# A mixture-of-experts stage in whole weight units: the down product moves behind the next slot's gate and up

## The chip, the cores and the metric

The kernel runs on one core of a Trainium2 chip. The metric is the device time of one execution in microseconds (us), the median of three runs. The weights lie in HBM in float32, and the result has to be of nearly float32 quality, which sets how the matrix products are made (below).

## The reference, cut to what matters

Two layers act on 512 latent tokens; the first also carries 256 context tokens, so its expert stage has 768 tokens and that of layer two 512. Each layer is a mixer (layer one: a gated linear recurrence beside differential attention; layer two: windowed attention) and then a routed mixture of 16 experts, of which every token takes two. The change is in this stage alone:

```python
D_MODEL = 1024; N_EXPERTS = 16; TOP_K = 2; D_EXPERT = 1024

def routed_moe(h2d, router_w, router_b, w_gate, w_up, w_down):
    aff = jax.nn.sigmoid(jnp.dot(h2d, router_w).astype(F32))
    ...                                  # two experts of the best group of four, normed weights wts
    def expert_block(args):              # a block: up to 128 rows of one expert e
        xblk, e = args
        hid = jax.nn.silu(xblk @ w_gate[e]) * (xblk @ w_up[e])
        return hid @ w_down[e]
    yb = lax.map(expert_block, (xb, block_e)).reshape(n_rows, d_)
    out = jnp.zeros((n_tok + 1, d_), F32).at[row_tok].add(yb * row_w[:, None])
```

Every expert's three matrices (1024x1024 float32, 4 MB each) are used in both layers: 192 MB a layer, read once.

## The kernel before, in words

**Slots.** The stage of a layer runs over 16 slots, one expert each. Slot 0 is an expert that is known before the routing; the others are ranked by load. A slot's number of rows is fixed when the kernel is built (`PLANS`): 128, 64, or 128 and a further block of 32. Rows that find no place go to a loop, `tc.For_i(0, n_ov)`, whose count `n_ov` is read at run time (`values_load(nov)`). With these inputs it runs zero times, but every engine loads the count and branches, and before that each waits until the other engines and all transfers that were issued so far are done.

**Weights.** A slot has 12 units of 1 MB, of 128 partitions x 2048: 4 of gate, 4 of up, 4 of down. SyncE (SP) issues their loads (`load_raw`) into raw buffers of several pools (`ROOM` gives the pools' sizes, the strings `FIRST` and `ROUND` name the pool for each unit in turn). A load waits until its buffer is free.

**Products.** For a block of 128 rows a unit is split into two float32r parts: ScalarE (ACT) writes `wh` (a copy, L193), VectorE (DVE) writes `wl` = raw - wh (L195), two such pairs of 1024 columns to a unit. TensorE (PE) then makes three products for each 128x512 piece, `mm3` (L208, L209, L210). So a 128-row slot has 96 of them for gate and up (on `xh`, `xl`) and 48 for down (on `hh`, `hl`), beside 16 transposes. A block of 64 or 32 rows takes the raw weights as they are (`thin`, L1219, on `xn`, then `hn`).

**Order in a slot.** Gate and up are made in two halves of 512 columns: steps 0 to 3 read all 8 units, two a step, for columns 0 to 511, and steps 4 to 7 read the same 8 units for columns 512 to 1023. A unit's raw buffer is free after the second. After each half `hidden` makes silu(gate) * up (L1336, L1337), transposes it on PE (L1201) and splits it into `hh` and `hl` (L1205, L1206). Steps 8 to 11 are the down product of the same slot, then `result` weights the rows and POOL stores them to `YD` (L1431). The rows of the next slot are gathered by POOL (`fetch`, L1184), transposed on PE and split in the slot before.

**Start and end.** 12 units are loaded ahead of the routing's result (`AHEAD`). After that step 15 (slot 0 and three steps of slot 1) the loop stands. Behind slot 14 the rows in YD are gathered for the output (`fetch_y`, L1131), slot 15 goes to the output by a product with a selection matrix (L1447).

Of the kernel before, what the change touches and what calls it, by code (L numbers as in the profile page):

```python
# [9 lines left out]
FT = mybir.dt.float32  # L10
FR = mybir.dt.float32r
# [20 lines left out]
ROOM = [(5, 1, 3), (2, 4, 1, 3)]  # L32
BRIEF = [True, False]
# [5 lines left out]
LOOP_POOL = [2, 3]  # L39


class Plan:
# [21 lines left out]
    Plan([(128,)] * 3 + [(64,), (128,)] * 6 + [(64,)]),  # L64
# [48 lines left out]
def body(tc, a):  # L113
# [8 lines left out]
    with ExitStack() as top:  # L122
# [996 lines left out]
        def ffn(li, nt, xs, keep, project, after_project, at_end):  # L1119
# [39 lines left out]
            with ExitStack() as es:  # L1159
# [31 lines left out]
                def loop_pool():  # L1191
                    return room[LOOP_POOL[li]]


# [28 lines left out]
                def run(experts, blocks, sizes):  # L1223
# [12 lines left out]

                    def gather(p, first, step):
# [3 lines left out]
                        def get():  # L1241
                            if in_loop:
                                p["ix"] = wk.tile([128, 1], I32, name="ix")
                                p["sw"] = wk.tile([128, 1], FT, name="sw")
                                V.tensor_copy(p["ix"], rowi[:, ds(b + NB - 1, 1)])
                                V.tensor_copy(p["sw"], roww[:, ds(b + NB - 1, 1)])
                                p["xg"] = fetch(p["ix"][:, 0:1])
                                return
                            p["sw"] = (roww if m == 128 else again[m][:, 1])[:, b:b + 1]
                            p["ix"] = (rowi if m == 128 else again[m][:, 0])[:, b:b + 1]  # L1250
                            p["xg"] = fetch(rowi[:m, b:b + 1], p["n"] % 2 == 0, m)

                        def turn(q):
# [3 lines left out]
                            if q == 0 and in_loop:  # L1257
                                p["xh"] = (keep if one else wk2).tile([128, 8, 128], FR, name=f"xhl{li}", tag="xl0" if one else "y", bufs=1 if one else 2)
                                p["xl"] = wk2.tile([128, 8, 128], FR, name="xll", tag="y", bufs=1 if one else 2)
                            elif q == 0:  # L1260
                                for x in ("xh", "xl"):
                                    p[x] = wk2.tile([128, 8, 128], FR, name=x, bufs=1 if one else 2)
# [14 lines left out]
                    slots, n = [], 0  # L1277
                    for s in range(len(experts)):
                        slots.append([])
                        for b, m in zip(blocks[s], sizes[s]):  # L1280
                            r0 = (b + NB - 1) * 128 if in_loop else b * 128
                            row = (lambda i, k, r0=r0: ds(r0, 128)) if in_loop else (lambda i, k, r0=r0: slice(r0 + i, r0 + i + k))
                            slots[-1].append(dict(b=b, m=m, n=n, row=row))
                            n += 1
                    total = 12 * len(slots)
                    ahead, raws, regs = {}, {}, {}

                    def expert(s):
                        e = experts[s]
                        if callable(e):  # L1290
                            e = regs[s] = regs[s] if s in regs else e()
                        return e

                    def load(u, eng=nc.sync, order=False):
                        s, q = divmod(u, 12)
                        w = (wg, wu, wd)[q // 4][ds(expert(s), 1)].rearrange("o (u p j) n -> p (o u) (j n)", p=128, j=2)
                        k = len(FIRST[li])
                        pool = 0 if in_loop else int(FIRST[li][u] if u < k else ROUND[li][(u - k) % len(ROUND[li])])
                        raw = load_raw(w[:, q % 4], loop_pool() if in_loop else wx if pool == 9 else room[pool], eng, order)
                        return raw.rearrange("p (j n) -> p j n", j=2)  # L1300

                    def part(m, kh, c):

                        w = (wg, wu)[m][ds(expert(0), 1)].rearrange("o (u p j) n -> p (o u) j n", p=128, j=2)
                        raw = loop_pool().tile([128, 2048], FT, name="raw", tag="raw").rearrange("p (k n) -> p k n", k=4)
                        for x in range(2):
                            nc.sync.dma_start(raw[:, 2 * x:2 * x + 2], w[:, 2 * kh + x, :, 512 * c:512 * c + 512])
                        return raw

                    def unit(u):  # L1310
                        if u not in raws:
                            raws[u] = ahead.pop(u) if u in ahead else load(u)
                        return raws[u]

                    def weights(i):
# [7 lines left out]
                        if in_loop:  # L1323
                            return split(part(m, kh, c)), []
                        rs = [unit(12 * s + 4 * m + 2 * kh + x) for x in range(2)]
                        return [w for r in rs for w in split(r[:, :, 512 * c:512 * c + 512])], rs

                    def hidden(p, c, step):

                        pg, pu = p["ps"]  # L1330

                        def vec():
                            if c == 0:
                                p["h"] = [wk.tile([128, 8, 128], FR, name=x, bufs=1) for x in ("hh", "hl")]
                            sg = wk.tile([128, 512], FT, name="sg", bufs=1 if one else 2)
                            S.activation(sg, pg, AF.Silu)  # L1336
                            V.tensor_mul(sg, sg, pu)  # L1337
                            p["sg"] = sg
# [4 lines left out]
                        def store():  # L1343
                            parts(p["pt"], *(x[:, 4 * c:4 * c + 4] for x in p["h"]))

                        if step is None:
                            vec()
                            turn()
                            store()
                        else:  # L1350
                            at(step, False, vec)
                            at(step, True, turn)
                            at(step + 1, False, store)

                    def hidden_thin(p, step):

# [595 lines left out]
```

## Time and profile before

| | |
|---|---|
| median of three runs | 2195.73 us (2192.98 to 2196.71) |
| the profiled execution | 2198.97 us, span 2197.3 us |
| granted TensorE clock, mean | 0.961 |
| PE, DVE, ACT busy | 91%, 65%, 52% of the span |
| DMA | 569.22 MB, 259 GB/s over the span |
| expert stage of layer one | about 581 us (first unit load) to 1261 us |
| expert stage of layer two | about 1609 us (first unit load) to 2197 us |

The profile is of one execution. It has rows of 40 equal slices of the span (each 54.9 us) with the busy share of each engine in tenths, the clock that PE was granted (1.00 is 2.4 GHz, half of it 1.2 GHz), and what the 16 DMA engines moved. The other views are a table of stretches of time, the waits of one engine by what ended them, and lists of instructions in order of time.

### The profile page before, as it was taken

How to read it: one execution, taken by the hardware profiler on the slowest of the kernel's cores; microseconds unless marked ns; L12 is line 12 of the kernel's file. 1: busy time of each engine (PE TensorE's matmuls, PEld its weight loads, DVE VectorE, ACT ScalarE, POOL GpSimd, SP SyncE). 2: the span in 40 equal slices, each digit the busy share in tenths (PEclk: the TensorE clock that was granted, in tenths of full speed). 3: DMA queues.
4: the chain of work that ended last, by engine and by line, in shares of the span. 5: the costliest groups of instructions: out<-in, count | busy, mean ns of one | idle time of the engine just before them, and what ended most of it. 6: DMA issues, size and time to landing. Idle time of an engine off the chain costs nothing. (4 is left out here: it accounts for less than half of the span.)

```text
span 2197.3 us, 31173 instructions
## 1 busy us (share of the span) xinstructions
PE 1997.5 (91%) x11439; PEld 1505.1 (68%) x11439; DVE 1429.6 (65%) x2283; ACT 1144.3 (52%) x1816; POOL 207.1 (9%) x269
## 2 busy tenths in 40 slices
PE   4899999998968999999999889999967999999996
PEld 2777898997746887767778467566745865556653
DVE  3656746667677987857789465565576954556653
ACT  5444474443235886757678262565335743354541
POOL 1211110000110000000000330000010000000002
PEclk8899999999978999999999989999988999999998
DMA  8865333213456899899989842440428999999996
GB/s 306 284 208 197 90 96 100 75 47 104 176 212 236 362 401 355 335 402 396 356 330 383 306 133 102 172 162 1 146 110 317 377 414 412 413 412 413 412 417 191
DMA packets 128230, 569.22 MB, mean 259 GB/s; under 512 B 12790, under 2 KB 48640, under 8 KB 72440
## 3 DMA queue, kind: packets, MB, share of 16 engines
q1 hardware_dynamic: 103104, 485.36, 56.7%
q0 software_dynamic: 17856, 66.71, 9.2%
q10 hardware_dynamic: 7112, 15.10, 2.1%
q8 instruction: 93, 1.52, 0.3%
q14 instruction: 65, 0.53, 0.1%
HBM read 540.01 MB, written 38.12 MB: 263 GB/s over the span
## 5 line engine op out<-in xcount | busy, mean ns | idle before, releaser
L195 DVE TENSOR_TENSOR wl<-raw,wh 128x1024 fp32r<-128x1024 f32 (+1 forms) x606 | 722.8, 1219 | 160.0 <-ACT wh L193 149.5
L193 ACT ACTIVATE wh<-raw 128x1024 fp32r<-128x1024 f32 (+1 forms) x606 | 629.6, 1054 | 269.8 <-PE acc L210 206.0
L209 PE MATMUL acc<-wl,xh 128*128 128x512 f32 x736 | 300.5, 408 | 35.5 <-DVE wl L195 32.5
L208 PE MATMUL acc<-wh,xh 128*128 128x512 f32 x736 | 296.8, 406 | 13.1 <-ACT wh L193 13.1
L210 PE MATMUL acc<-wh,xl 128*128 128x512 f32 x736 | 295.1, 401 | 0.0
L208 PE MATMUL acc<-wh,hh 128*128 128x512 f32 (+2 forms) x716 | 271.7, 379 | 4.3 <-ACT hh L476 3.9
L210 PE MATMUL acc<-wh,hl 128*128 128x512 f32 (+2 forms) x716 | 265.1, 371 | 0.3 <-DVE hl L477 0.3
L209 PE MATMUL acc<-wl,hh 128*128 128x512 f32 (+2 forms) x716 | 264.8, 370 | 0.0
L209 PEld LDWEIGHTS acc<-wl,xh 128*128 128x128 f32 x736 | 143.2, 195 | 76.1 <-DVE wl L195 37.1
L208 PEld LDWEIGHTS acc<-wh,xh 128*128 128x128 f32 x736 | 143.2, 195 | 57.3 <-ACT wh L193 22.5
L210 PEld LDWEIGHTS acc<-wh,xl 128*128 128x128 f32 x736 | 143.2, 195 | 29.4 <-DVE xl L1206 0.5
L208 PEld LDWEIGHTS acc<-wh,hh 128*128 128x128 f32 x716 | 137.1, 191 | 25.4 <-ACT hh L476 4.3
L210 PEld LDWEIGHTS acc<-wh,hl 128*128 128x128 f32 x716 | 136.1, 190 | 21.7 <-DVE hl L477 0.8
L209 PEld LDWEIGHTS acc<-wl,hh 128*128 128x128 f32 x716 | 136.7, 191 | 18.3
L1219 PE MATMUL acc<-raw,xn 128*64 128x512 f32 (+1 forms) x832 | 141.3, 529 | 0.0
L1219 PEld LDWEIGHTS acc<-raw,xn 128*64 128x64 f32 (+1 forms) x832 | 48.0, 128 | 86.8 <-issue 77.5
L1184 POOL DMA_INDIRECT xg<-H,rowi x32 | 42.0, 1314 | 637.0 <-PE tp L1201 570.4
L1219 PE MATMUL acc<-raw,hn 128*64 128x512 f32 (+1 forms) x416 | 75.4, 540 | 10.6 <-DMA raw<-in_moe_w_down_dram 6.8
L1363 DVE TENSOR_TENSOR sg<-sg,acc 128x512 f32<-128x512 f32 (+1 forms) x11 | 7.0, 638 | 119.5 <-PE acc L1219 119.5
L152 POOL TENSOR_TENSOR rr<-rv,mhalf 128x1 f32<-128x1 f32 (+1 forms) x54 | 37.1, 687 | 481.4 <-DVE rv L150 463.7
L1205 ACT ACTIVATE xh<-tp 128x512 fp32r<-128x512 f32 x46 | 27.0, 588 | 99.2 <-PE tp L1201 99.2
L1047 DVE TENSOR_REDUCE mx<-big 128x1 f32<-128x512 f32 (+1 forms) x64 | 48.1, 756 | 37.1 <-PE big L1045 36.4
(416 smaller groups left out, 3296.4 us busy)
## 6 DMA issues: line engine op xcount, KB each, us to landing
raw<-in_moe_w_gate_dram SPq DMA_DIRECT2D x128, 1024.0 KB, 10.7
raw<-in_moe_w_up_dram SPq DMA_DIRECT2D x128, 1024.0 KB, 13.0
raw<-in_moe_w_down_dram SPq DMA_DIRECT2D x127, 1024.0 KB, 14.5
raw<-in_ada_w_dram SPq DMA_DIRECT2D x48, 1024.0 KB, 6.2
YD<-y POOLq DMA_DIRECT2D x23, 512.0 KB, 8.1
YD<-YD POOLq DMA_DIRECT2D x21, 512.0 KB, 11.9
raw<-in_even_w_in_dram SPq DMA_DIRECT2D x40, 256.0 KB, 4.5
raw<-in_even_w_in_dram SPq DMA_DIRECT2D x12, 512.0 KB, 4.6
```

The lines of the kernel that those rows point to most:

```text
L152: G.tensor_tensor(r, v, mhalf[:, :n], OP.pow)
L193: S.activation(v[0], src, AF.Copy)
L195: newest[0] = V.tensor_sub(v[1], src, v[0].bitcast(FT))
L208: T.matmul(o, xh, wh, start=start, stop=False)
L209: T.matmul(o, xh, wl, start=False, stop=False)
L210: T.matmul(o, xl, wh, start=False, stop=stop)
L1047: V.tensor_reduce(mx[:, i:i + 1], ps[:, :n], AX.X, OP.max, negate=True)
L1184: i = G.indirect_dma_start(out=xg[:rows], out_offset=None, in_=H[:, :], in_offset=bass.IndirectOffsetOnAxis(ap=ix, axis=0))
L1205: S.activation(oh, pt, AF.Copy)
L1219: T.matmul(ps[m * r:m * r + m, :n], x, w[:, n * r:n * r + n], start=start, stop=stop, tile_position=(0, m * r))
L1363: V.tensor_mul(sg, sg, pu[:, :8 * m])
```

## The change

A step is one whole unit: each of its two 128x1024 parts goes into two PSUM banks, one for each half of the columns (`thick`). The steps stand in the list `seq`: gate and up of slot s (8 steps), then down of slot s-1 (4 steps); at the end down of slot 14, gate and up of slot 15, down of slot 15. `hh`, `hl` and `hn` get two buffers; `xh` and `xl`, of which layer one had two, get one. SP loads 11 units ahead in layer one (8 of gate and up, 3 of down) and 12 in layer two; before, POOL issued the twelfth of layer one. The loop stands after step 4 of slot 0, and its body is written out on its own (`overflow`). Layer two's slots were 128 rows x 3, (64, 128) x 6, 64; they are 128, (64, 128) x 6, 128 x 2, 64: as many of each size.

```diff
-ROOM = [(5, 1, 3), (2, 4, 1, 3)]
-FIRST = ["000091113331100001111291", "0093110022224440011002222"]
-ROUND = ["00009111112", "934440011002222"]
-AHEAD = [(range(11), range(11, 12)), (range(12), range(0))]
-LOOP_AFTER = [range(15, 21), range(15, 25)]
+ROOM = [(5, 1), (2, 1, 4, 2)]
+FIRST = ["9200001192000011111", "920000114492000033331144920000"]
+ROUND = ["92000011111", "33331144920000"]
+AHEAD = [[*range(8), *range(16, 19)], [*range(8), *range(16, 20)]]
+LOOP_STEP = 4
...
-    Plan([(128,)] * 3 + [(64,), (128,)] * 6 + [(64,)]),
+    Plan([(128,)] + [(64,), (128,)] * 6 + [(128,)] * 2 + [(64,)]),
...
+                def thick(ps, kk, hi, lo, ws, w=512):
+                    wh, wl = ws
+                    for x in range(2):
+                        cs = slice(w * x, w * x + w)
+                        mm3(ps[x], hi[:, kk], lo[:, kk], wh[:, cs], wl[:, cs], kk == 0, kk == 7)
...
+                        if s == 15:
+                            seq += [(14, q) for q in range(8, 12)]
+                        seq += [(s, q) for q in range(8)]
+                        if 0 < s < 15:
+                            seq += [(s - 1, q) for q in range(8, 12)]
+                    seq += [(15, q) for q in range(8, 12)]
...
                     def weights(i):
-                        s, q = divmod(i, 12)
-                        m, kh, c = q // 2 % 2, q % 2, q // 4
-                        if slots[s][0]["m"] < 128:
-                            return [], [unit(i)]
-                        if q >= 8:
-                            return split(unit(i)), [unit(i)]
-                        rs = [unit(12 * s + 4 * m + 2 * kh + x) for x in range(2)]
-                        return [w for r in rs for w in split(r[:, :, 512 * c:512 * c + 512])], rs
+                        raw = ahead.pop(i) if i in ahead else load(i)
+                        return split(raw) if slots[seq[i][0]][0]["m"] == 128 else [], raw
...
-                                p["h"] = [wk.tile([128, 8, 128], FR, name=x, bufs=1) for x in ("hh", "hl")]
+                                p["h"] = [wk.tile([128, 8, 128], FR, name=x) for x in ("hh", "hl")]
...
-                            turns.append(12 * s - 5 + 2 * x if one else max(12 * s - 5 + 2 * x, 10))
-                            gather(p, max(turns[-3] + 2, 16) if p["n"] > 1 else 4, turns[-1])
+                            turns.append(6 if s == 1 else g - 3 + 2 * x)
+                            gather(p, LOOP_STEP if p["n"] == 1 else max(turns[-3] + 2, 9), turns[-1])
...
+                            for x, p in enumerate(slots[s]):
+                                if q == 7 and p["m"] == 128:
+                                    hidden(p, 0, i + 1)
+                                    hidden(p, 1, i + 2)
...
-                steps(11)
-                early_units[0](LOOP_AFTER[li])
-                steps(15)
+                steps(LOOP_STEP)
                 n_ov = nc.values_load(nov[0:1, 0:1], min_val=0, max_val=OVMAX)
                 in_loop = all_in_wx[0] = True
                 with tc.For_i(0, n_ov, 1) as j:
-                    finish(run([lambda: nc.sync.value_load(eoi[0:1, ds(j, 1)], min_val=0, max_val=15)], [[j]], [(128,)]))
+                    overflow(j)
                 in_loop = all_in_wx[0] = False
+                if one:
+                    steps(10)
+                    gates()
```

In `weights`, before, `m`, `kh` and `c` are gate or up, the half of the rows, and the half of the columns.

A scheduler sets the final order on each engine. The first place is SP at the loop in layer two. Before, these rows stand there: the 12 units ahead, the expert number of slot 1 (`esi`), 9 loads of slot 1 and 4 of slot 2 (left out), and then the count.

```order
L164 DMA raw<-in_moe_w_gate_dram 128x2048 x4
L164 DMA raw<-in_moe_w_up_dram 128x2048 x4
L164 DMA raw<-in_moe_w_down_dram 128x2048 x4
L1757 TENSOR_LOAD esi
...
L164 DMA raw<-in_moe_w_gate_dram 128x2048
L1812 TENSOR_LOAD nov
L1814 COMPARE_AND_BRANCH
```

Now the count stands right behind the 12 units, and the expert number of slot 1 with its 8 loads of gate and up comes behind the loop:

```order
L162 DMA raw<-in_moe_w_gate_dram 128x2048 x4
L162 DMA raw<-in_moe_w_up_dram 128x2048 x4
L162 DMA raw<-in_moe_w_down_dram 128x2048 x4
L1781 TENSOR_LOAD nov
L1783 COMPARE_AND_BRANCH
...
L1781 ISA x2
L1736 TENSOR_LOAD esi
L1736 ISA x2
L162 ISA
L162 DMA raw<-in_moe_w_gate_dram 128x2048
```

In layer one the count moved in the same way on SP. On PE it moved up by nine steps: 72 products of slot 0 stand ahead of it in layer one (gate, and half of up) and 96 in layer two (all of gate and up of slot 0), where before the count stood in slot 1.

The second place is DVE in a 128-row slot of layer one, early in the stage. Before, the four products for `sg` and `hl` of a slot lie in two places, 14 and 6 splits apart:

```order
L195 TENSOR_TENSOR wl<-raw,wh 128x1024 x14
L1337 TENSOR_TENSOR sg<-sg,acc 128x512
L195 TENSOR_TENSOR wl<-raw,wh 128x1024 x2
L1206 TENSOR_TENSOR hl<-tp,hh 128x512
L195 TENSOR_TENSOR wl<-raw,wh 128x1024 x6
L1206 TENSOR_TENSOR xl<-tp,xh 128x512
L1337 TENSOR_TENSOR sg<-sg,acc 128x512
L195 TENSOR_TENSOR wl<-raw,wh 128x1024 x2
L1206 TENSOR_TENSOR xl<-tp,xh 128x512
L1206 TENSOR_TENSOR hl<-tp,hh 128x512
```

Now 16 splits stand in a row, and the six others all lie among the next eight, those of the four down units:

```order
L193 TENSOR_TENSOR wl<-raw,wh 128x1024 x16
L1380 TENSOR_TENSOR sg<-sg,acc 128x512
L193 TENSOR_TENSOR wl<-raw,wh 128x1024 x2
L1380 TENSOR_TENSOR sg<-sg,acc 128x512
L193 TENSOR_TENSOR wl<-raw,wh 128x1024 x2
L1200 TENSOR_TENSOR hl<-tp,hh 128x512
L193 TENSOR_TENSOR wl<-raw,wh 128x1024 x2
L1200 TENSOR_TENSOR xl<-tp,xh 128x512
L1200 TENSOR_TENSOR hl<-tp,hh 128x512
L193 TENSOR_TENSOR wl<-raw,wh 128x1024 x2
L1200 TENSOR_TENSOR xl<-tp,xh 128x512
```

## Rows read from the trace of the kernel before

**Rows 1.** The page: what the DMA moved in 40 slices of the span.

```profile
GB/s 306 284 208 197 90 96 100 75 47 104 176 212 236 362 401 355 335 402 396 356 330 383 306 133 102 172 162 1 146 110 317 377 414 412 413 412 413 412 417 191
```

**Rows 2.** Windows of stages: length, busy us of each engine, clock, DMA share, GB/s.

```profile
708.00:1223.00 515.00, 510.65 (x2587) 396.98 (x2588) 418.51 (x400) 377.74 (x424) 33.19 (x38) 0.99 0.93 370
...
1752.00:2109.00 357.00, 338.69 (x1507) 208.35 (x1506) 194.60 (x201) 157.16 (x180) 24.16 (x27) 0.98 1.01 413
```

**Rows 3.** Windows: one 128-row slot of layer one.

```profile
778.20:813.30 35.10, 35.10 (x162) 28.84 (x161) 31.80 (x30) 28.77 (x33) 2.02 (x2) 1.00 1.00 403
```

**Rows 4.** Windows: one of four like pairs, a 128-row and a 64-row slot, layer two.

```profile
1848.00:1913.20 65.20, 60.68 (x268) 38.04 (x267) 36.19 (x37) 29.10 (x33) 4.46 (x5) 0.97 1.01 414
```

**Rows 5.** What SP's loads wait for, 1750 to 2140 us: total, times, longest.

```profile
SPq L164 <- DVE wl L195: 143.9, 71, 12.9
SPq L164 <- PE acc L1219: 63.9, 41, 4.5
```

**Rows 6.** PE in time, layer one: slot 0's 72nd product, then the loop.

```profile
679.58 0.39 PE L210 MATMUL acc<-wh,xl 128*128 128x512 f32 x1
...
707.69 0.80 PE L209 MATMUL acc<-wl,xh 128*128 128x512 f32 x1 [2.93 <-issue]
```

**Rows 7.** The tile xg, 640 to 760 us: the gathers of a slot's rows.

```profile
DMA to landing us min/median/max: 4.6/6.6/9.8
```

**Rows 8.** What PE waits for, 708 to 1223 us: total, times, longest.

```profile
PE acc L208 <- ACT wh L193: 2.2, 3, 1.7
PE acc L209 <- DVE wl L195: 1.5, 2, 0.8
```

**Rows 9.** PE in time, slot 14 and 15 of layer two.

```profile
2128.16 0.39 PE L208 MATMUL acc<-wh,xh 128*128 128x512 f32 x1
2130.88 0.40 PE L208 MATMUL acc<-wh,xh 128*128 128x512 f32 x1
...
2147.16 0.39 PE L209 MATMUL acc<-wl,hh 128*128 128x512 f32 x1
2150.87 0.39 PE L210 MATMUL acc<-wh,hl 128*128 128x512 f32 x1
2151.19 3.65 PE L1219 MATMUL acc<-raw,xn 128*64 128x512 f32 x16
...
2169.36 7.09 PE L1219 MATMUL acc<-raw,hn 128*64 128x512 f32 x32 [0.47 <-ACT hn L1210]
```

**Rows 10.** DVE groups in 708 to 1223 us: count, busy us, mean ns.

```profile
L195 DVE TENSOR_TENSOR wl<-raw,wh 128x1024 fp32r<-128x1024 f32 x310 | 372.0, 1223 | 76.9 <-ACT wh L193 71.4
L1206 DVE TENSOR_TENSOR hl<-tp,hh 128x512 fp32r<-128x512 f32 x26 | 17.8, 685 | 0.2 <-ACT hh L1205 0.2
```

**Rows 11.** POOL in time, the end of layer one.

```profile
1257.00 2.35 POOL L1832 TENSOR_TENSOR ye<-ye,g 128x1024 f32<-128x1024 f32 x1 [9.50 <-DMA ye<-YD,dse]
```

**Rows 12.** PE in time, layer two: slot 0's gate and up end, the loop.

```profile
1661.10 0.40 PE L210 MATMUL acc<-wh,xl 128*128 128x512 f32 x1
1675.47 0.40 PE L210 MATMUL acc<-wh,hl 128*128 128x512 f32 x1
1683.49 0.79 PE L208 MATMUL acc<-wh,xh 128*128 128x512 f32 x1 [7.62 <-ACT wh L193]
1693.77 0.79 PE L209 MATMUL acc<-wl,xh 128*128 128x512 f32 x1 [6.09 <-DVE wl L195]
```

**Rows 13.** Windows of layer two: around the loop, from first to last load.

```profile
1680.00:1690.00 10.00, 3.72 (x7) 2.07 (x7) 2.45 (x2) 3.17 (x4) 0.31 (x1) 0.66 0.61 248
1690.00:1704.00 14.00, 10.23 (x37) 8.28 (x38) 8.70 (x8) 7.61 (x9) 1.76 (x2) 0.76 0.61 208
...
1650.00:2155.00 505.00, 469.02 (x2074) 311.70 (x2073) 307.13 (x308) 247.25 (x277) 30.86 (x36) 0.97 0.98 398
```

**Rows 14.** POOL in time, the end of layer two.

```profile
2152.34 0.57 POOL L1431 DMA_DIRECT2D YD<-y  x1 [41.33 <-DVE y L1417]
2171.18 1.55 POOL L1131 DMA_INDIRECT xs<-YD,dse  x1 [1.01 <-DMA xs<-YD,dse]
```

More of the change, by code (lines that the diff above doesn't have):

```diff
@@ new lines, in y_tile, with pieces @@
+                def y_tile():
+                    return wk2.tile([128, 8, 128], FT, name="y", bufs=1 if one else 2).rearrange("p a b -> p (a b)")
+                def pieces(p):
+                    if p["m"] == 128:
+                        return [(p["d"][c], slice(0, 128), slice(512 * c, 512 * c + 512), slice(512 * c, 512 * c + 512)) for c in range(2)]
+                    m, n = p["m"], 8 * p["m"]
+                    return [(p["d"][m * r:m * r + m], slice(m * r, m * r + m), slice(0, n), slice(n * r, n * r + n)) for r in range(128 // m)]
@@ L1285, in run @@
[L1285 to L1313, printed above, removed]
@@ new lines, in vec, with turn @@
+                            p["sg"] = sg = wk.tile([128, 512], FT, name="sg", bufs=1 if one else 2)
+                            S.activation(sg, p["g"][c], AF.Silu)
+                            V.tensor_mul(sg, sg, p["u"][c])
+                        def turn():
+                            p["pt"] = turned(p["sg"])
+                        at(step, False, vec)
+                        at(step, True, turn)
+                        at(step + 1, False, lambda: parts(p["pt"], *(x[:, 4 * c:4 * c + 4] for x in p["h"])))
@@ L1338, in vec, with hidden_thin @@
+                    def hidden_thin(p, step):
+                        m = p["m"]
+                        def vec():
+                            sg = wk.tile([128, 512], FT, name="sg", bufs=1 if one else 2)[:, :8 * m]
+                            S.activation(sg, p["g"], AF.Silu)
+                            V.tensor_mul(sg, sg, p["u"])
                             p["sg"] = sg
@@ L1514, in run @@
-                            for p in ps_:
-                                if p["m"] == 128 and q in (3, 7):
-                                    hidden(p, c, None if in_loop else i + 1)
-                                elif p["m"] < 128 and q == (3 if whole else 7):
-                                    if whole:
-                                        hidden_thin(p, i + 1)
-                                    else:
-                                        at(i, True, lambda p=p: hidden_thin(p, None))
-                                elif q == 9 and last and not in_loop:
+                            s, q = seq[i]
@@ new lines, in run @@
+                            m, k0, last = q // 4, 2 * (q % 4), s == 15
+                            key = "gud"[m]
+                            for p in slots[s]:
+                                if q % 4 == 0 and p["m"] == 128:
+                                    p[key] = [acc(), acc()]
+                                elif q % 4 == 0 and p["m"] == 64:
+                                    p[key] = acc()
+                                elif q % 4 == 0:
+                                    n = 8 * p["m"]
+                                    if m != 1:
+                                        p["bank"] = tp([128, 2 * n])
+                                    p[key] = p["bank"][:, n * (m == 1):n * (m == 1) + n]
+                                for k in range(2):
+                                    if p["m"] == 128:
+                                        thick(p[key], k0 + k, *(p["h"] if m == 2 else (p["xh"], p["xl"])), ws[0][k])
+                                    else:
+                                        thin(p[key], (p["h"] if m == 2 else p["x"])[:, k0 + k], ws[1][:, k], k0 + k == 0, k0 + k == 7)
@@ L1523, in run @@
                                     pick(p, i + 1)
                                 elif q == 11:
[L1525 removed]
+                                    (direct if last else result)(p, i + 1)
                             ws = nws
```

248 lines of the change are left out of this document (103 added, 145 removed).

## The prediction

> **What bounds the kernel now.** I read the page's slices first: in the expert stage of layer two the DMA moves an even 412 to 417 GB/s slice after slice, in that of layer one 330 to 402 [rows 1]. The windows by stage then say which engine goes with it. Layer one, from the loop to the end of slot 14, 708 to 1223 us: PE is busy 510.65 of 515 us, DVE 418.51, the DMA has a share of 0.93. Layer two, 1752 to 2109: PE 338.69 of 357, the DMA 1.01 at 413 GB/s [rows 2]. So layer one is bound by PE and layer two by the loads. Neither has much slack behind the bound: a 128-row slot of layer one lasts 35.1 us, all of it PE, with DVE at 31.8 and the DMA share at 1.00 [rows 3]. A pair of a 128-row and a 64-row slot in layer two lasts 65.2 us with PE at 60.7 and the DMA at 414 GB/s; these are 24 units, 2.72 us each [rows 4]. The waits of SP in layer two agree: it waits for buffers that DVE and PE still hold (143.9 and 63.9 us) [rows 5], and the DMA is full all the same.
>
> The two layers have to be summed apart. In layer one only what PE does or waits for counts, in layer two only when the last load lands and what still stands behind it.
>
> **The sum is made against the span, 2197.3 us.** The profiled execution took 2198.97, its span and 1.7 around it; the median of the runs is 2195.73, 3.2 lower. Differences are put on the median. Less than 0.2%, 4.4 us, can hardly be told from no change.
>
> **Layer one, the loop.** Before, PE stood at the loop until 707.69 with 15 steps done, and its 72nd product started at 679.58 [rows 6]. The loop now stands right behind that product: six steps. The wait at the old loop ended with the store of slot 0's rows; no store is under way now, so I let PE go on at 684, 4 us after the product. To reach the 15 steps it then needs nine steps of 12 products at 0.23 us, 24.8, and 24 transposes, some 3.2: 712.2. That is +4.5. From below it is 0 (the loop is passed at 679.8), from above +8 (it has the last loads to wait for).
>
> The gather of slot 1's rows is now issued behind the loop. Such gathers land 4.6 to 9.8 us after their issue, in the median 6.6 [rows 7]. PE has 16 products ahead of the transposes, 3.7 us. The wait is 2 to 6 us less what the old place cost (nothing); I take +3.5, ends 0 and +6. Slot 1's loads also come behind the loop, but four down units of slot 0 (11 us of PE) and 16 products lie ready for PE, and the first load needs about 5 us.
>
> **Layer one, the slots.** The work is the same: as many products, splits and transposes. What goes is the burst of two units a step. PE lost 2.2 + 1.5 us to it between 708 and 1223, where a 128-row slot follows the 64-row one, and 0.7 at other places [rows 8]. With one unit a step I take all 4.4 as gone; ends -4.4 and 0.
>
> What may come is a longer spacing of products. In gate and up before, the bank in PSUM stays the same over many products: 12 spacings from 2128.16 to 2130.88, 0.227 us each. In down the bank changes after every three: 16 from 2147.16 to 2150.87, 0.232 [rows 9]. With `thick`, gate and up change in the same way. 96 products x 5 ns x 13.5 slots is 6.5 us if the bank is the cause and 0 if `hh` against `xh` is only chance. I take half, +3.
>
> Here the Trainium skill has a figure. "TensorE: Matmul & The Clock Gate", in "Wait — 56ns, not 53.3ns?", gives one start-to-start time of 215.7 ns for 512 columns at the full clock, whatever the bank. By it this term would be 0 and the sum 3 us lower; both spacings of the trace are longer than the page's, and they differ from each other, so the measurement decides.
>
> Six DVE operations now lie among the last eight splits of a slot (the order of DVE, above). Eight splits at 1.22 us and six at 0.69 are 13.9 us [rows 10]; PE needs for the same four steps 48 x 0.232 and 12 to 16 transposes, some 12.7. DVE falls 1.2 us behind. The first 16 splits take 19.5 where PE has 22, so it regains that, and `wh` and `wl` hold two units, 5.5 us of PE. Cost 0, covered by these two units; without that cover 1.2 a slot. The hidden rows of a slot are wanted only eight steps after they are made, so nothing waits for them.
>
> Layer one's end follows slot 14: the store of its rows, the eight gathers, and POOL's products, which start when the last gather of the first tile has landed at 1257.00 [rows 11]. The order is the same as before there. Cost 0. **Layer one in all: +4.5 + 3.5 - 4.4 + 3 = +6.6, from -4.4 to +20.**
>
> **Layer two, the start of the loads.** Before, PE ended gate and up of slot 0 at 1661.1, down at 1675.5, then waited 7.6 us, started slot 1 and waited 6.1 more at the loop [rows 12]. Behind it the loads ran dry: 248 and 208 GB/s in 1680 to 1704 [rows 13]. From 1650 to 2155 the loads moved 398 GB/s x 505 us, 201 MB, which at 414 would be 485 us: 20 us of the DMA were lost.
>
> Now SP stands at the loop until the 96 products of slot 0 are done, 1661, and the loop is passed. First load about 1665, full rate from 1667 on. There is no second dry place behind it, since the loop is past, and the 201 MB take 485 us: the last unit lands at about 2152 instead of 2155. So the loads alone give 3 us. PE meanwhile has down of slot 0 to do, 11 us, and then waits for slot 1; that costs nothing as long as the loads set the pace.
>
> **Layer two, the end.** This is the main term. Before, slot 14 (128 rows) ended at 2151.2, and only then slot 15's 64 rows began, 25 us of products with the last ending at 2176.5 [rows 9], although its last unit had landed about 2155. The reason is the half columns: the first four steps want eight units, 21.7 us of the DMA, for 11 us of products, and PE then has 22 us of products for four units. It waits in the first half and is late in the second. Now a step wants one unit, 2.72 us of the DMA, and has 12 products, 2.75, so PE follows the loads. After the last 64-row slot before them three 128-row slots stand in a row; each takes PE 35.1 where the loads need 32.6, a lag of 7.5 us at the end. Slot 14's last unit lands 12 units before the last one, 2152 - 32.6 = 2119.4; with the lag and some 3 us for split and products slot 14 ends at about 2130, 21 earlier.
>
> Two chains then end the kernel. Slot 15's down waits for the last unit: 2152, and about 2 us of products; from the end of the products to the end of the span it was 2197.3 - 2176.5 = 20.8, so 2175. The other is POOL: slot 14's store, eight gathers, the sum. It was 2197.3 - 2151.2 = 46.1 from the end of slot 14, of which 20.4 from the store's issue to the end of the last gather's [rows 14]. From 2130 that is 2176. The gathers then lie beside full loads until 2152, where before only 4 us of loads were left; I add 3. The end comes at 2179, **-18 us**. Ends: -8 (PE lags by as much as ten more us, or the gathers are slowed by as much) and -30 (loads at 420 GB/s, no lag).
>
> **Sum: +6.6 - 18 = -11.4, 2184.3 us.**
>
> **The rivals.**
> - *Slower: layer one pays for DVE.* If the two units of cover are not there, because a split waits for its buffer of `wh` or a transpose for its PSUM bank, each of the 14 slots of 128 rows loses the 1.2 us that DVE lies behind, or more: the six operations wait for PE's transposes, and PE's next step for the splits behind them. From 1.3 us a slot layer one loses 18, and with its +6.6 the kernel is slower; at 2 us a slot, 28, the time is 2212. Speaking for it: DVE is busy 31.8 of 35.1 us, and the DMA is full as well. Against it: 3.3 us a slot of DVE are free.
> - *Layer two gains little.* The gathers beside full loads, or PE's lag, keep the end within 5 us of where it was. Time 2195.73 + 6.6 - 5 = 2197. Speaking for it: before, the gathers had nearly free queues. Against it: the same gathers in layer one ran beside slot 15's loads, and took as long.
> - *Better.* No term for the spacing, the loop passed at once, the loads at 420 GB/s: layer one -1, layer two -26, 2169.
> - *The clock.* If changing banks lets PE fall to half its clock (spacing 0.43), layer one would lose 0.2 us a product; 96 in one slot in ten are 27 us, about 2211. The trace has PE at a granted 1.00 over a whole slot whose down part changes banks [rows 3], so 0.03. The Trainium skill speaks of it: "TensorE: Matmul & The Clock Gate", "A second HAM failure mode: psum-queue depth-cycling", tells of a kernel whose clock swings since it changes PSUM banks in each iteration.
> - *It does nothing* can't be: loop, order and loads move.
>
> **How the numbers follow.** Forecast 0.50, better 0.15, little in layer two 0.15, slower by DVE 0.17, the clock 0.03. The forecast has its own range, 2175 to 2193. Faster by over 0.2%, below 2191.3: nearly all of the forecast (0.47), better, a little of the third, 0.65. Within 0.2%: 0.14. Slower, above 2200.1: 0.21. The range leaves 1 in 10 on either side, 2166 to 2203.
>
> **What would show it.** In the profile after: the loop passed by PE near 684 and 1664; SP's first load of layer two behind the loop near 1665 and no stretch below 380 GB/s after 1670; no PE wait in layer one after slot 1; the spacing of gate and up 0.227 or 0.232; slot 14's store near 2131 + 6.6, and the last products of slot 15 20 to 25 us ahead of the end. The forecast is wrong if PE waits for `wl` once in each slot of layer one, or if slot 14 of layer two ends later than 10 us before the last load's landing.

## The result and the profile after

The changed kernel takes 2209.3 us in the median of five runs (2207.75 to 2213.68), the kernel before 2196.71 beside it (2192.98 to 2199.25). The ratio is 1.0062, interval 1.0047 to 1.0078: 0.6% slower, where 2184 was forecast. All ratios below are against the kernel before on the same chip.

The page of the changed kernel, its span and what the DMA moved in 40 slices of 55.1 us:

```profile
span 2205.8 us, 31127 instructions
...
GB/s 312 282 210 186 92 104 100 75 47 104 100 241 243 421 411 308 328 421 417 316 327 384 300 144 77 192 135 1 31 258 218 413 413 420 414 413 420 411 420 226
```

The expert stage of layer two begins in the 30th slice. Against [rows 1] the 29th to 31st are the ones to see: 31, 258 and 218 GB/s where before it was 146, 110 and 317. From the 32nd on it is as even as before. The windows say the same of both layers (length, busy us of PE, PEld, DVE, ACT and POOL, clock, DMA share, GB/s):

```profile
703.00:1208.00 505.00, 501.75 (x2531) 383.23 (x2530) 406.74 (x388) 365.88 (x414) 31.21 (x36) 1.00 0.94 371
...
1632.00:1678.00 46.00, 27.45 (x123) 21.35 (x123) 37.84 (x93) 18.16 (x18) 1.18 (x2) 0.78 0.46 192
...
1760.00:2130.00 370.00, 347.12 (x1551) 226.76 (x1548) 230.74 (x234) 189.55 (x214) 20.37 (x26) 1.00 1.01 416
```

Layer one is PE's as before [rows 2], layer two the loads', but 46 us at the start of layer two run at 192 GB/s. In the middle of layer two SP no longer waits for buffers, as in [rows 5], but nearly only for earlier loads to land:

```profile
SPq L162 <- DMA raw<-in_moe_w_down_dram: 103.4, 52, 2.7
SPq L162 <- DMA raw<-in_moe_w_up_dram: 101.5, 48, 3.6
SPq L162 <- DMA raw<-in_moe_w_gate_dram: 98.2, 45, 3.2
SPq L162 <- DVE wl L193: 2.7, 7, 0.8
```

So buffers come free early enough, as the whole units were to do it. Where the time went is seen when the span is cut at six instructions that stand in both programs: the first transposes of the router's columns in each layer (tp<-ct,mr; in layer two the last of them), the first product of slot 0 on xh, and the first product of slot 15 on xn, which is the end of slot 14. In us, each from one profiled execution:

| | start to router 1 | to slot 0 | to end of slot 14 | to router 2 | to slot 0 | to end of slot 14 | to the end | median of runs |
|---|---|---|---|---|---|---|---|---|
| before | 592.9 | 60.2 | 569.8 | 368.8 | 39.2 | 520.3 | 46.1 | 2196.7 |
| changed | 595.4 | 63.6 | 573.6 | 371.2 | 45.6 | 507.3 | 49.1 | 2209.3 |
| forecast, difference | 0 | 0 | +6.6 | 0 | 0 | -21 | +3 | |
| measured, difference | +2.5 | +3.4 | +3.8 | +2.4 | +6.4 | -13.0 | +3.0 | |

The first column is ahead of everything that the change touches; over 14 profiles it lies between 589.0 and 599.2 without any order, so its 2.5 us are scatter. Programs that are alike in layer one (the changed kernel, e2 and e7 below) differ there by up to 0.9 us in the second column and 1.5 in the third, so smaller differences tell nothing. The columns behind the first add up to +6.0, where the forecast has -11.4. What is left of the 12.6 us between the medians is scatter of the profiled executions: before was profiled at 2198.97, 2.3 above its median, the changed kernel at 2207.75, 1.6 below.

Four columns are more than 2 us worse than forecast: the two from the router to slot 0 (3.4 and 6.4), slots 0 to 14 of layer two (8.0), and the end of layer one (2.4). Layer one's slots are 2.8 better. The loads ahead are the first thing that differs. SP in order of time, the units ahead in layer one and in layer two; start, time from the first issue to the end of the last, count. The changed kernel:

```profile
584.38 52.52 SPq L162 DMA_DIRECT2D raw<-in_moe_w_gate_dram  x4
636.99 2.16 SPq L162 DMA_DIRECT2D raw<-in_moe_w_up_dram  x4
...
1620.63 1.32 SPq L162 DMA_DIRECT2D raw<-in_moe_w_gate_dram  x3
1622.04 2.68 SPq L162 DMA_DIRECT2D raw<-in_moe_w_up_dram  x4
1624.76 7.59 SPq L162 DMA_DIRECT2D raw<-in_moe_w_down_dram  x4
```

The kernel before:

```profile
580.81 10.56 SPq L164 DMA_DIRECT2D raw<-in_moe_w_gate_dram  x4
598.61 29.91 SPq L164 DMA_DIRECT2D raw<-in_moe_w_up_dram  x4
...
1554.59 0.33 SPq L164 DMA_DIRECT2D raw<-in_moe_w_gate_dram  x1
1562.56 21.06 SPq L164 DMA_DIRECT2D raw<-in_moe_w_up_dram  x4
1586.21 23.69 SPq L164 DMA_DIRECT2D raw<-in_moe_w_down_dram  x4
```

Before, layer one's are issued over some 60 us. Of layer two's twelve three are issued at 1452.6 and the others over 55 us, the last at 1609.6 (the time that the table ahead of the prediction gives for the first). Now all but the first come in one bunch of 8 to 12 us, right where slot 0's rows are gathered. In layer two PE's lists show what waits behind that bunch. The kernel before:

```profile
1629.16 1.95 PE L1201 MATMUL tp<-ct,xg 128*128 128x128 f32 x8 [5.39 <-DMA xg<-H,ix]
```

The changed kernel:

```profile
1637.30 0.24 PE L1682 MATMUL tp<-val,oh 128*128 128x2 bf16 x4 [3.69 <-DMA raw<-in_moe_w_up_dram]
1647.64 1.95 PE L1195 MATMUL tp<-ct,xg 128*128 128x128 f32 x8 [10.09 <-DMA xg<-H,ix]
1649.42 0.80 PE L206 MATMUL acc<-wh,xh 128*128 128x512 f32 x1
...
1675.34 0.40 PE L208 MATMUL acc<-wh,xl 128*128 128x512 f32 x1
1685.23 1.22 PE L1195 MATMUL tp<-ct,xg 64*128 64x64 f32 x8 [9.49 <-DMA xg<-H,rowi]
```

The gather of slot 0 keeps PE for 10.1 us instead of 5.4, and after slot 0's 96 products PE waits 9.5 us for the gather of slot 1, which POOL could issue only behind the loop.

### The profile page after: what moved, and what is told of

Read it like the earlier page. It is cut to its first block, busy times and chain, and to the rows that moved or that the text cites. A ratio compares the mean times of both kernels' runs of the same rounds, so it can differ in the third digit from the quotient of the medians.

```text
span 2205.8 us, 31127 instructions
## 1 busy us (share of the span) xinstructions
PE 1996.7 (91%) x11439; PEld 1494.0 (68%) x11439; DVE 1421.3 (64%) x2283; ACT 1137.5 (52%) x1816; POOL 202.2 (9%) x269
## 5 line engine op out<-in xcount | busy, mean ns | idle before, releaser
L193 DVE TENSOR_TENSOR wl<-raw,wh 128x1024 fp32r<-128x1024 f32 (+1 forms) x606 | 713.2, 1215 | 123.8 <-ACT wh L191 109.1
L191 ACT ACTIVATE wh<-raw 128x1024 fp32r<-128x1024 f32 (+1 forms) x606 | 620.2, 1053 | 265.1 <-PE acc L208 161.1
L207 PE MATMUL acc<-wl,xh 128*128 128x512 f32 x736 | 293.6, 399 | 10.7 <-DVE wl L193 10.7
L206 PE MATMUL acc<-wh,xh 128*128 128x512 f32 x736 | 259.0, 397 | 1.7 <-ACT wh L191 1.7
L206 PE MATMUL acc<-wh,hh 128*128 128x512 f32 (+2 forms) x716 | 255.7, 378 | 4.7 <-ACT hh L474 3.9
L207 PEld LDWEIGHTS acc<-wl,xh 128*128 128x128 f32 x736 | 140.1, 190 | 49.2 <-DVE wl L193 20.0
L207 PEld LDWEIGHTS acc<-wl,hh 128*128 128x128 f32 x716 | 136.9, 191 | 30.0 <-DVE wl L193 10.1
L1213 PE MATMUL acc<-raw,xn 128*64 128x512 f32 x576 | 130.9, 600 | 8.1 <-DMA raw<-in_moe_w_up_dram 8.1
L1182 POOL DMA_INDIRECT xg<-H,rowi x32 | 39.1, 1223 | 756.1 <-PE tp L1195 561.5
L1213 PEld LDWEIGHTS acc<-raw,xn 128*64 128x64 f32 x576 | 39.3, 138 | 92.1 <-issue 68.2
L1213 PE MATMUL acc<-raw,hn 128*64 128x512 f32 x288 | 69.2, 614 | 18.3 <-DMA raw<-in_moe_w_down_dram 17.3
L1396 DVE TENSOR_TENSOR sg<-sg,acc 128x512 f32<-128x512 f32 x9 | 6.2, 687 | 119.2 <-PE acc L1213 119.2
L1195 PE MATMUL tp<-ct,xg 128*128 128x128 f32 (+2 forms) x272 | 44.9, 294 | 29.1 <-DMA xg<-H,ix 19.6
## 6 DMA issues: line engine op xcount, KB each, us to landing
YD<-YD POOLq DMA_DIRECT2D x22, 512.0 KB, 12.1
```

What stands on the lines that cost most here:

```text
L191: S.activation(v[0], src, AF.Copy)
L193: newest[0] = V.tensor_sub(v[1], src, v[0].bitcast(FT))
L206: T.matmul(o, xh, wh, start=start, stop=False)
L207: T.matmul(o, xh, wl, start=False, stop=False)
L1182: i = G.indirect_dma_start(out=xg[:rows], out_offset=None, in_=H[:, :], in_offset=bass.IndirectOffsetOnAxis(ap=ix, axis=0))
L1195: T.transpose(pt[:, i], v[:, i // 2, i % 2], ident[:m, :m])
```

## The experiments

Theory A: the loads ahead come late, and the routing and slot 0 pay for it. Theory B: the loop's new place costs, since all loads of slot 1 and its gather wait behind it. Theory C: the new order of rows in layer two, three 128-row slots at its end, makes PE late for the last loads. The table gives the columns of the table above that move.

| run | to slot 0, layer 1 | slots, layer 1 | to slot 0, layer 2 | slots, layer 2 | to the end | median | ratio (interval) |
|---|---|---|---|---|---|---|---|
| e1_pools | 63.8 | 575.4 | 42.4 | 508.5 | 49.0 | 2205.12 | 1.0036 (1.0018 to 1.0054) |
| e2_plan | 64.2 | 575.1 | 45.4 | 501.2 | 52.8 | 2202.95 | 1.0028 (1.0017 to 1.0039) |
| e3_no_loop | 64.3 | 577.5 | 45.6 | 492.6 | 47.4 | 2192.44 | 0.9976 (0.9965 to 0.9986) |
| e4_before_no_loop | 59.6 | 572.0 | 38.9 | 517.7 | 46.1 | 2198.67 | 1.0010 (0.9995 to 1.0025) |
| e6_pools_all | 58.2 | 572.8 | 44.9 | 506.2 | 49.1 | 2199.69 | 1.0015 (1.0001 to 1.0030) |
| e67_early_units | 58.4 | 575.7 | 45.3 | 498.7 | 49.2 | 2195.34 | 0.9989 (0.9978 to 1.0001) |
| e7_two_early | 64.5 | 573.9 | 45.4 | 503.7 | 48.6 | 2204.22 | 1.0032 (1.0019 to 1.0046) |
| e5_before_plan | 59.3 | 569.5 | 39.1 | 516.5 | 46.1 | 2198.21 | 0.9997 (0.9981 to 1.0014) |
| e8_six_early | 58.1 | 573.0 | 42.1 | 496.0 | 48.5 | 2186.21 | 0.9939 (0.9923 to 0.9956) |
| e9_gather | 58.1 | 572.9 | 42.4 | 491.7 | 48.5 | 2180.09 | 0.9920 (0.9891 to 0.9948) |
| e9c_gather_l1 | 58.1 | 572.9 | 42.3 | 493.1 | 49.0 | 2181.09 | 0.9933 (0.9908 to 0.9958) |
| e10_gather_plan | 57.9 | 574.3 | 42.4 | 484.5 | 53.0 | 2176.67 | 0.9907 (0.9873 to 0.9941) |

**e1_pools**, the buffers of the first units exchanged (digit = pool; 0 the four shared ones, 9 the split buffer, 2 a pool of one):

```diff
-FIRST = ["9200001192000011111", "920000114492000033331144920000"]
+FIRST = ["0000921192000011111", "000092114492000033331144920000"]
```

> The changed kernel, but the first units ahead take the buffers that are free early (the pool of four that all stages share), and the two that come free only when the projection ends come fifth and sixth. Theory A, late loads: the changed kernel is slow since ten of its units ahead wait at SP's head for one buffer, come in one bunch at 636 us (layer one) and 1621 (layer two), and slot 0's gather and the routing stand behind them. Then four units a layer land before the routing, slot 0's first product of layer two comes 5 to 7 us earlier, that of layer one 2, and the time falls by 7 to 9, to about 2201. Theory B, the loop's new place, and theory C, three 128-row slots at the end of layer two, expect 2 us at most: about 2208.

Layer two gave back 3.2 of the 6.4 us, layer one nothing. In layer one the unit in the pool of one stood sixth, and it and those behind it still came together at 639 us.

**e2_plan**, the rows of layer two as before.

```diff
-    Plan([(128,)] + [(64,), (128,)] * 6 + [(128,)] * 2 + [(64,)]),
+    Plan([(128,)] * 3 + [(64,), (128,)] * 6 + [(64,)]),
```

> The changed kernel with layer two's rows as before: 128 x 3, (64, 128) x 6, 64. Theory C: the end of slot 14 lies 21 us behind the landing of its last unit since PE (35 us a slot) falls behind the loads (30 us a slot, 2.5 us a unit) in three 128-row slots in a row; with only one at the end it lies 10 behind, and the time falls by 8 to 10, to about 2200. Theories A and B: no gain; the three slots are then behind the loop, where PE has 35 us of work a slot while the loads fill up, so the lag is only paid at another place: 2205 to 2213.

Slots 0 to 14 of layer two take 6.1 us less, the end 3.7 more: 2.4 in all by these columns, 6.4 by the medians. Theory C holds for its mechanism, and for a part of its size.

**e3_no_loop** and **e4_before_no_loop**, each kernel without its loop.

```diff
-                n_ov = nc.values_load(nov[0:1, 0:1], min_val=0, max_val=OVMAX)
-                in_loop = all_in_wx[0] = True
-                with tc.For_i(0, n_ov, 1) as j:
-                    overflow(j)
-                in_loop = all_in_wx[0] = False
```

> The changed kernel without the loop for rows that find no place (left out: rows of overflow, of which these inputs have none). Theory B: the loop right behind slot 0's first products costs 6 us of PE in layer one and makes all loads of slot 1 wait until 1678 in layer two, with 9.5 us of PE for slot 1's gather; without it the time falls by 15 or more, to 2194 or less. Theory A: the loads ahead stay late, so only the 6 us of layer one and a part of the 9.5 go: 2198 to 2203. To be read beside the kernel before without its loop.

> The kernel before without the loop (left out: rows of overflow, of which these inputs have none). Its loop cost PE 2.9 us in layer one and 6.1 in layer two, and the loads ran at 208 to 248 GB/s for 24 us there, 11 us of the DMA. If the loop costs the kernel before less than the changed one (theory B) it gains 3 to 6 us here, 2191; if it costs both about the same (theories A and C), 9 to 13, 2185.

The changed kernel gains 17 us, all of it in layer two (slots 14.7, end 1.7). The kernel before gains nothing in its median, 2.6 in those slots, less than either theory gave it. The window that read 192 GB/s in the changed kernel reads, without the loop:

```profile
1632.00:1678.00 46.00, 26.14 (x123) 20.42 (x124) 38.19 (x103) 19.61 (x21) 2.23 (x2) 0.77 1.01 409
```

This is theory B, and its place is the DMA: PE does the same in both windows. Without the loops the change itself takes 25.1 us from layer two's slots (517.7 to 492.6). Both programs without a loop have slower products (last section). In layer two that is 5 ns on 8 x 96 products of gate and up, 3.8 us, and either of the two gains, 14.7 and 2.6, may be larger by up to this; in layer one it hides the gain.

**e6_pools_all**, the pools in the order in which their places come free, and ten units ahead in layer one instead of eleven.

```diff
-FIRST = ["9200001192000011111", "920000114492000033331144920000"]
-ROUND = ["92000011111", "33331144920000"]
-AHEAD = [[*range(8), *range(16, 19)], [*range(8), *range(16, 20)]]
+FIRST = ["0000911100009111112", "009211004400921133330044"]
+ROUND = ["00009111112", "00921133330044"]
+AHEAD = [[*range(8), *range(16, 18)], [*range(8), *range(16, 20)]]
```

> The changed kernel with its raw buffers in the order in which their places come free, in both layers (as the kernel before has them: the four shared buffers first, in layer two two of them, then the split buffer, the pool of one, the pool of two); layer one loads 10 units ahead instead of 11. Theory A: late loads ahead cost 3.5 us in layer one and 6.4 in layer two between the routing and slot 0's first product. The run with only the first pools exchanged mended 3 of layer two and nothing of layer one, where the pool of one buffer still stood in SP's way at the fifth unit; here layer one should gain 2 to 3.5 and layer two 5 to 6: 2200 or less. Theory B, the loop alone: no more than the 4 us of that run, 2205.

Layer one: 58.2, so 5.4 less, 2 better than the kernel before. Layer two only 0.7: there the order of e1, with the four shared buffers first and the pool of one sixth instead of fourth, was the better one. The median fell by 9.6, to 0.15% above the kernel before. Theory A holds in layer one for the whole of the 3.4 us, in layer two (e1) for half of the 6.4.

**e67_early_units** and **e7_two_early**: the first units of slot 1 issued ahead of the loop (e67 with e6's pools, four units in each layer; e7 with nothing else, two units in layer two).

```diff
                 steps(LOOP_STEP)
+                early_units[0](EARLY_UNITS[li])
                 n_ov = nc.values_load(nov[0:1, 0:1], min_val=0, max_val=OVMAX)
...
+                    early_units.append(lambda us: ahead.update({u: load(u) for u in us}))
```

> As the run with all pools in order, and the first four units of slot 1 are issued ahead of the loop in both layers (their buffers come free with slot 0's first products). Theory B: what the loop costs is the DMA standing still in layer two from the last unit ahead to the loop's end, 1632 to 1678; four units are 10 us of that, and slot 1's gate lies ready behind the loop: 8 to 10 us less than the run with the pools alone, in layer two only; about 2191. Theory A: equal to that run within 2 us.

> The changed kernel as it is, with only two units of slot 1 of layer two issued ahead of the loop, into the two raw buffers that stand empty there; nothing else. Theory B: two units are 5 us of the DMA; 4 to 5 us faster, 2204 to 2205. Theory A: none, 2209.

Two units take 3.6 us from layer two's slots, four take 7.5 (against e6). The medians fell by 5 and 4. In layer one the four units did harm, +2.9: PE then waits 11.5 us behind the loop for slot 1's gather.

**e5_before_plan**, the kernel before with the new order of rows (the diff of e2 the other way round).

> The kernel before with the rows of layer two as in the changed one: 128, (64, 128) x 6, 128 x 2, 64. Theory C: three 128-row slots at the end make PE late for the last loads here too: 4 to 8 us slower, about 2203. If the order of rows matters only by where PE has work for the loads' start, it gives some of the dry time behind the loop back to the loads: same within 3 us.

No difference in the median (the slots of layer two took 3.8 us less in one profile). So theory C is a cost of the changed kernel alone; that PE ends late in either order with half columns would explain it, and was not looked into.

**e8_six_early**: e6 in layer one, e1's order in layer two, six early units in layer two, none in layer one. **e9_gather**: also slot 1's gather ahead of the loop; **e9c_gather_l1** with four early units in layer one too; **e10_gather_plan**: e9 with e2's rows.

```diff
-                            gather(p, LOOP_STEP if p["n"] == 1 else max(turns[-3] + 2, 9), turns[-1])
+                            gather(p, 3 if p["n"] == 1 else max(turns[-3] + 2, 9), turns[-1])
...
-                    xg = keep.tile([128, D], FT, name=f"xg{li}", tag="xl0") if other else kp.tile([128, D], FT, name="xg")
+                    xg = y_tile() if in_loop else keep.tile([128, D], FT, name=f"xg{li}", tag="xl0") if other else kp.tile([128, D], FT, name="xg")
```

> Pools in the order in which they come free (layer one as in the run with all pools in order, layer two with the four shared buffers first), and six units of slot 1 of layer two, none of layer one, issued ahead of the loop. Theory B (the DMA stands still from the last unit ahead to the loop's end): six units are 15 us of DMA, 5 more than four; but with four the loads had ceased to bind, PE waited in layer two for the loop and slot 1's gather, 12.4 us, so no more than 2 to 3 us come from here, and 3 from the earlier units ahead of layer two: 2190 to 2193. If the loads still bind: 2187.

> As the run with six early units, and slot 1's gather is issued ahead of the loop in both layers (the loop's body gathers into the buffer of y instead). Theory B in its second half: what is left of the loop's price is PE's wait for that gather, which is issued behind the loop together with a burst of loads (11.5 us in layer one and 12.4 in layer two with early units): most of both goes, 12 to 15 us in all, to 2177 to 2182. If the barrier itself is the price (PE has to wait for the gather's landing at the loop instead): 3 us or less, 2188.

> As the run with the early gather, and four units of slot 1 of layer one too are issued ahead of the loop. If layer one has only PE as its bound once the gather is early, the same within 2 us; if its start still waits for slot 1's units, 2 to 4 us faster.

> As the run with the early gather, with layer two's rows as before (128 x 3, (64, 128) x 6, 64). Theory C: in the changed order of rows slot 14 ends 21 us behind its last unit's landing; with one 128-row slot at the end, 10: 4 to 6 us faster. Against it: with early units PE and not the loads binds the end of layer two, and PE's work is the same in both orders: the same within 3 us.

SP of e8 in layer two, in order of time: the units ahead spread over some 30 us, then six of slot 1 where the DMA had nothing to do:

```profile
1586.09 3.46 SPq L163 DMA_DIRECT2D raw<-in_moe_w_gate_dram  x2
1589.59 26.17 SPq L163 DMA_DIRECT2D raw<-in_moe_w_up_dram  x4
1615.80 2.37 SPq L163 DMA_DIRECT2D raw<-in_moe_w_down_dram  x4
1635.76 9.22 SPq L163 DMA_DIRECT2D raw<-in_moe_w_gate_dram  x4
1647.10 4.33 SPq L163 DMA_DIRECT2D raw<-in_moe_w_up_dram  x2
```

PE's first work behind the loop in layer two, e8:

```profile
1677.84 1.22 PE L1196 MATMUL tp<-ct,xg 64*128 64x64 f32 x8 [11.81 <-DMA xg<-H,rowi]
```

And e9:

```profile
1667.22 1.17 PE L1196 MATMUL tp<-ct,xg 64*128 64x64 f32 x8 [3.00 <-DVEq L1786]
```

The wait of 11.8 us is 3.0, now for the loop itself. Only 4.3 of these 8.8 us show in the slots, and the median fell by 6; in 1700 to 2100 us the loads run at 413 to 415 GB/s in both programs, so that they bind there is likely. With layer one's four units the same comes out (e9c), and with the old rows 7.2 us less in the slots and 4.5 more at the end (e10). e10 is the fastest, 0.9% below the kernel before, and still has the loop. Between the medians of e9 and e10 lie 3.4 us, less than the width of their intervals.

## Why the prediction was wrong

The columns of the changed kernel are 17.4 us worse than forecast: 9.8 from the router to slot 0 in both layers, 8.0 in layer two's slots, 2.4 at the end of layer one, less 2.8 in layer one's slots. Two steps failed by much: a term put at nothing, and a lag that was half of what it is.

**The loads ahead, not in the sum.** The step that failed first is the one that isn't there: the sum begins at the loop and takes all up to slot 0's first product as unmoved. The order rows of SP showed the same 12 units, and I took them as loaded at the same time. The strings give it away: the second unit takes a pool of one that comes free only when the projection ends (SP waits 50.8 us for PE there in layer one, 47.5 in layer two), SP works in order, and nine or ten units stand behind it. Measured 3.4 + 6.4 us; with the pools in order layer one's part goes wholly and more (e6), layer two's by half (e1, e8).

**"So the loads alone give 3 us": this step held.** By the forecast slot 14's last unit lands 488.4 us after slot 0's first product (2119.4 less 1631); it landed 486.6 after it (2136.0 less 1649.4). The loads' standstill at the loop, 17 us by the forecast, was thus in the sum. What the forecast didn't ask is whom such a standstill costs. Before, PE was late in the stage anyhow, and the lost DMA time cost it little: without the loop its slots gain 2.6 us. Now that PE follows the loads, DMA time lost at the start comes back at the end: 14.7 us. The same mechanism that brings the gain makes the loop dear, and this is where e8 and e9 found time.

**The end of slot 14, -21, measured -13.0.** The mechanism is right: without loops it is -25.1. The failed step is the lag of 7.5 us, with 3 for split and products. Slot 14's last unit landed at 2136.0, and the slot ended at 2156.7, 20.7 later. PE was already 6.6 us behind when slot 12's gate and up ended (last unit landed at 2051.9, last product at 2058.5), and lost 14.1 more up to slot 14's end. The loads there came at 2.63 us a unit (32 from 2051.9 to 2136.0) instead of the 2.72 of [rows 4], which hold stores and gathers too: 3.2 us in 36 units. Another 3.2 are PE's waits for `wl` in 2060 to 2136, which the forecast had at nothing. e2, which removes the three slots in a row, gets 6 us back. With early loads the lag is 20.0 us in e9 (landed at 2109.6, ended at 2129.6) and with the old rows 12.1 in e10 (2111.1, 2123.2).

**The end, +3 from the gathers beside full loads:** measured +3.0, but the size is luck. The eight gathers take as long as before, 16.7 us from the first issue to the end of the last (before 16.5). It is POOL's wait for the store of the zero row ahead of them that grew, from 2.8 to 8.3 us. From the last gather's landing to the end of the span 3.0 us are won back (13.4 instead of 16.4), which was not looked into. The kernel before, then the changed one:

```profile
2156.27 1.65 POOL L1131 DMA_INDIRECT xs<-YD,dse  x1 [2.81 <-DMA YD<-zero]
...
2158.04 0.53 POOL L1255 DMA_DIRECT2D YD<-y  x1 [9.65 <-DVE y L1241]
...
2167.35 1.64 POOL L1129 DMA_INDIRECT xs<-YD,dse  x1 [8.25 <-DMA YD<-zero]
```

**Layer one's slots, +6.6, measured +3.8.** PE at the loop of layer one, changed kernel:

```profile
684.17 0.40 PE L207 MATMUL acc<-wl,xh 128*128 128x512 f32 x1
690.60 0.80 PE L208 MATMUL acc<-wh,xl 128*128 128x512 f32 x1 [6.03 <-issue]
```

It goes on 6.6 us later than I put it, of which 6.0 is the later start of slot 0 (659.0 against 653.1). The 108 products of the nine steps that are then left end at about 720.6, after 30 us where the forecast had 28. That is 12.9 after [rows 6], and less the late start +6.9; forecast +4.5. The gather's +3.5 was nothing, since PE came back so late. Of the 4.4 us of waits [rows 8] 3.1 are still there:

```profile
PE acc L206 <- ACT wh L191: 1.7, 1, 1.7
PE tp L1195 <- DVE sg L1396: 0.9, 1, 0.9
PE acc L207 <- DVE wl L193: 0.5, 1, 0.5
```

That is -1.3. The products give another -1.0: 0.230 us instead of 0.232 in down (672 of them, -1.7), 0.2280 instead of 0.2275 in gate and up (some 1250, +0.7). Together +4.6; the 0.8 to the measured +3.8 is less than the column's scatter. The same rows answer the rival that I put on the other side: no 128-row slot of layer one pays for DVE's bunched operations; the two units of cover hold there. The term of +3 for the spacing was near 0: below. The clock stayed at 1.00.

**The end of layer one, 0, measured +2.4.** The last two loads of slot 15 were issued at 1247.3 and 1248.0 instead of 1226.6 and 1242.6, and PE waited 17.3 us for them where it had waited 6.8; e6 has only 9.9 us of it, in two waits, and comes to layer two's router just 0.4 us sooner, so it isn't this wait that sets the end. What the 2.4 us are was not tried.

## What to carry to other kernels

A change that lets an engine follow the loads more closely makes the time in which the loads stand still dear, here 14.7 us for the same loop that cost 2.6 before: price such a hole by who waits after the change, not by what it cost before. Where units are loaded ahead in program order, read from the allocation when each buffer's place comes free, since the first late one holds all that stand behind it. A barrier is cheap where loads are already issued past it and the next gather has landed; with six loads and the gather moved ahead of it (e9) layer two's slots take 491.7 us, as long as in e3 without any loop, 492.6. Another place for the barrier in the changed kernel was not tried.

## What the runs showed of the hardware

The spacing of the products is not a matter of the PSUM bank. In the changed kernel, whose products change the bank after every three, or after every one or two where the scheduler pairs them, gate and up take 0.226 us here, and the down products of slot 14 take 0.227:

```profile
2085.01 0.39 PE L208 MATMUL acc<-wh,xl 128*128 128x512 f32 x1
...
2089.99 0.39 PE L208 MATMUL acc<-wh,xl 128*128 128x512 f32 x1
...
2150.47 0.39 PE L208 MATMUL acc<-wh,hl 128*128 128x512 f32 x1
...
2151.83 0.39 PE L208 MATMUL acc<-wh,hl 128*128 128x512 f32 x1
```

From 2085.01 to 2089.99 are 22 spacings, from 2150.47 to 2151.83 six; before, gate and up took 0.227 with one bank over many products and down 0.232 [rows 9]. Not every down product of the changed kernel is as fast: some take 0.227, some 0.232, the mean over layer one is 0.230. And without the loop (e3) the gate and up products, the same instructions with the same banks, take 0.232, as ten from 899.68 to 902.00 show:

```profile
899.68 0.40 PE L206 MATMUL acc<-wh,xh 128*128 128x512 f32 x1
...
902.00 0.39 PE L207 MATMUL acc<-wl,xh 128*128 128x512 f32 x1
```

So does the kernel before without its loop. In the kernel before and in the changed one, too, the gate and up products of slot 0 take 0.233 in both layers. In layer one 5 ns on some 1250 products of gate and up are 6 us, and 2.5 ns on 672 of down 1.7: that is most of why e3's slots take 3.9 us more there though 6 us of waiting are gone, and a part of why e4 gains nothing. What sets the two values was not found; both are at a granted clock of 1.00. The Trainium skill, "TensorE: Matmul & The Clock Gate" in "Wait — 56ns, not 53.3ns?", gives one figure for 512 columns, 215.7 ns, and names no bank. That the bank doesn't matter the runs bear out, but 215.7 ns none of them reaches.

Behind the loop of layer one PE started its first product at 690.6, though DVE did at 686.5 and SP issued loads from 686.9; the profile names no releaser for these 4 us, and they were not looked into.
